# Folding the last quarter of a down projection into seven half-size products, in a hybrid encoder layer on one core

## The chip, the core and the metric

The kernel runs on one core of one Trainium2 chip. A core has a TensorE for matrix products (PE in the profile, PEld for its weight loads), a VectorE (DVE), a ScalarE (ACT), a GpSimd (POOL) and a SyncE (SP), which here only issues DMA transfers. Products are accumulated in the eight banks of PSUM; everything else lies in SBUF, in 83 slots of 128 x 512 fp32 and some smaller buffers. The metric is the device time of one execution in microseconds, lower is better.

## The reference, cut to what matters

One layer, 512 tokens by 1024 channels, fp32. The first half (norm, one input projection, a two-direction state-space scan, windowed attention, gates, an output projection) is not changed in what it computes, and only small edits of the diff touch it. The second half is the channel mixing:

```
h = rmsnorm(x, pre_mlp_norm)
f = square(relu(h @ w_mlp_in)) @ w_mlp_out      # w_mlp_in 1024 x 4096, w_mlp_out 4096 x 1024
x = x + rmsnorm(f, post_mlp_norm)
```

## The kernel before

**Three passes for a product.** A matrix product in near-fp32 precision is made of three passes in a rounded 32-bit type: both operands are split into a high part (rounded, by ACT) and a low part (the difference, by DVE or POOL), and `mm3` (L404) multiplies high by high, high by low and low by high into one bank. Weights come by DMA into raw tiles; ACT makes the high part (L473, or L1474 for the folded products) and POOL the low part in pieces of 256 columns (L477, L1477). Three buffers hold split weights (`SPL`).

**Quanta.** The program is a list of quanta (`Quantum`, L332), each a group of matmuls with its chunks of weights; `run_quanta` (L502) loads and splits ahead. `at(q, fn)` (L427) places other work beside quantum q. The instructions written out this way are then put in order by a planner (`Planner`, L92). It takes their dependences, an estimated cost for each, and due times counted back from the TensorE's own order (`deadlines`, L246), plays the program through, and fixes each engine's order with dependences (`chain`, L489). `depend` (L164) treats every two accesses to one PSUM bank as ordered, and also makes the first use of a tile wait for the first use of the tile that held the buffer's tag before. `next_matmul` (L126) tries to stay with one kind of matmul, since going from 128-wide to 64-wide tiles costs time. The 64-wide kind are pairs that write the two halves of a bank; the scan's `yd` (L1100 on) and the attention values use them.

**The MLP.** The up projection has 32 quanta of 24 matmuls, one for each block of 128 hidden channels (`up_quantum`, L1396; `up_done`, L1336, takes relu and square). The down projection is done by quarters of the hidden dimension. In a quarter the product is 512 tokens x 1024 hidden by 1024 hidden x 1024 outputs. Seen as 2 x 2 blocks, it takes eight block products directly, or seven with sums of blocks:

```
A (2x2) by B (2x2):  S2 = A21 + A22 - A11, S1 = A21 + A22, S3 = A11 - A21, S4 = A12 - S2
                     T2 = B22 - B12 + B11, T1 = B12 - B11, T3 = B22 - B12, T4 = T2 - B21
```

Here token halves are A's rows and output halves are B's columns. Each block product is 24 matmuls of 128 x 128 by 128 x 512 (two row blocks u of 128 tokens, four k, three passes). The first three quarters (`FOLDED = 3`) do it with seven products (`folded_quanta`, L1427 on). `combine` (L1362) makes the sums of A from two up blocks, `operand` the sums of B on DVE, from raw weight tiles. Three of the seven share a bank X and add up in it, two share Y, and A12 (bank Z) and A22 with T4 (bank W) have one to themselves. After each product `gather` (L1506 on) adds the bank into the outputs' accumulators `acc` (L1512), with a minus for A22 T4. Between the seven products of a quarter lie the up quanta of the next.

**The last quarter** has no up quanta left. It is unfolded (`down_quanta`, L1514 on): two output halves j, each four row blocks t by 24 matmuls, 192 matmuls for the two, the last row block of the second half in two pieces of 256 columns (24 more, shorter, matmuls). Its weights come as eight chunks of 512 KB. `down_done` (L1548 on) finishes a row block: add `acc` (L1557), square and sum on ACT (L1559), the running mean on DVE (L1562, L1564), the product with the norm's gain (`ag`, L1568), the power -1/2 on POOL (L1571), the scaled sum with x (L1575) and the store (L1576).

**Three places further ahead.** At the start 10 and then 8 matmuls on zeros run on TensorE while the inputs land (`WARM`), with the turn of a gain vector between them. `dt_math` (L718) evaluates log(1 + e) by a series with terms to 1/19. `k_done` (L786) splits K and writes each part to both halves of the partitions; both copies of the low part are made from the bank.

## Time and profile before

| | |
|---|---|
| median of 3 runs | 1101.49 us (1101.03 to 1101.82) |
| the profiled execution's own time | 1102.23 us |
| its span, from the first to the last instruction | 1100.4 us |
| granted TensorE clock, mean | 0.999 |
| DVE, ACT, POOL busy | 65%, 57%, 70% |
| bytes moved, mean rate | 128.12 MB, 116 GB/s |

The span is what the profile's clock covers; the execution's own time has 1.8 us more around it. "Busy" of an engine is a share of the span. Matmuls overlap: each row of one shows a length of about 0.39 us, but they start 0.227 us apart, so rates are read from starts. An idle time in square brackets behind a row is the time that the engine stood before it, with the work that ended it.

### The profile page before, as it was taken

Reading aid. Unit: us, or ns where it says so; the run is one execution under the profiler, and the core shown is the slowest. Engines: PE = TensorE matmul, PEld = TensorE weight load, DVE = VectorE, ACT = ScalarE, POOL = GpSimd, SP = SyncE. Lnnn points to the kernel's source line nnn. Section 1 sums busy time; section 2 is a strip of 40 time slices with the busy share of each in tenths; the row PEclk is TensorE's granted clock in tenths of the full one; section 3 lists DMA queues with packets and bytes.
Section 4 is the critical chain, followed back from the end, with each engine's and each line's share of the span. In section 5 each row is a group of like instructions: output and inputs, shape, how many; then the busy total and the mean of one; then the engine's idle time right before and its main releaser. Section 6 shows DMA issues by size and latency. Waiting matters only on the chain.

```text
span 1100.4 us, 16692 instructions
## 1 busy us (share of the span) xinstructions
PE 1087.9 (99%) x5679; PEld 912.4 (83%) x5679; DVE 710.3 (65%) x1242; ACT 627.2 (57%) x1345; POOL 771.0 (70%) x944
## 2 busy tenths in 40 slices
PE   9999999999999999999999999999999999999997
PEld 8878888888888878888888888889888888888886
DVE  5577787688687687777887753434655556564236
ACT  6466677677777667586779532323555444444331
POOL 3546667557668788898999776511679889898841
PEclk9999999999999999999999999999999999999999
DMA  7434434543454536354645564513312522523232
GB/s 203 126 94 111 117 92 111 140 106 101 114 123 124 145 96 168 97 148 126 165 129 148 142 171 125 170 53 98 113 39 77 172 58 78 171 58 97 64 108 77
DMA packets 206921, 128.12 MB, mean 116 GB/s; under 512 B 10170, under 2 KB 191930, under 8 KB 206835
## 3 DMA queue, kind: packets, MB, share of 16 engines
q1 hardware_dynamic: 206675, 126.98, 41.7%
q8 instruction: 45, 0.74, 0.3%
q14 instruction: 41, 0.34, 0.1%
q10 hardware_dynamic: 160, 0.07, 0.0%
HBM read 124.60 MB, written 2.42 MB: 115 GB/s over the span
## 4 chain that ended last, share of the span: by engine, by line
PE 63%; DVE 1%; issue 0%; ACT 0%; POOLq 0%; POOL 0%; DVEq 0%
PE pp L398 46%; PE ps L398 16%; PE ps L402 1%; DVE m L1095 0%; DVE m L1094 0%; DVE x L1575 0%; DVE rf L1089 0%; ACT junk L1559 0%; DVE acc L1557 0%; POOLq L1656 0%; POOL frs L1571 0%; DVE cb L1083 0%; DVEq L1656 0%; DVE frs L1564 0%; DVEq L1095 0%
## 5 line engine op out<-in xcount | busy, mean ns | idle before, releaser
L477 POOL TENSOR_TENSOR wl<-wr,wh 128x256 fp32r<-128x256 f32 (+1 forms) x511 | 442.0, 894 | 188.4 <-ACT wh L473 180.0
L398 PE MATMUL pp<-h,wh 128*128 128x512 f32 (+1 forms) x1728 | 527.9, 388 | 1.7 <-DVE KL L794 1.7
L398 PEld LDWEIGHTS pp<-h,wh 128*128 128x128 f32 x1728 | 319.1, 188 | 66.7 <-issue 4.2
L398 PE MATMUL pp<-h,wl 128*128 128x512 f32 (+1 forms) x856 | 332.1, 388 | 0.0
L473 ACT CAST wh<-wr 128x1024 fp32r<-128x1024 f32 (+1 forms) x141 | 146.9, 1043 | 162.7 <-PE pp L398 111.4
L398 PEld LDWEIGHTS pp<-h,wl 128*128 128x128 f32 x856 | 160.8, 188 | 32.1 <-issue 0.2
L1477 POOL TENSOR_TENSOR wl<-wd,wh 128x256 fp32r<-128x256 f32 x144 | 117.1, 849 | 13.6 <-ACT wh L1474 12.2
L398 PE MATMUL ps<-wl,fh 128*128 128x512 f32 (+1 forms) x192 | 73.0, 380 | 0.0
L398 PE MATMUL ps<-wh,fl 128*128 128x512 f32 (+1 forms) x192 | 73.0, 380 | 0.0
L398 PE MATMUL ps<-wh,fh 128*128 128x512 f32 (+1 forms) x192 | 73.0, 380 | 0.0
L1092 ACT ACTIVATE n<-cb,tables 128x128 f32<-128x128 f32 x128 | 49.1, 392 | 20.5 <-DVE cb L1083 17.8
L1474 ACT CAST wh<-wd 128x512 fp32r<-128x512 f32 x72 | 41.5, 619 | 31.3 <-PE ps L398 19.8
L924 DVE SCALAR_TENSOR_TENSOR u<-pp,cv,u 128x510 f32<-128x510 f32 (+1 forms) x64 | 47.7, 745 | 7.8 <-ACT u L920 6.7
L1088 ACT ACTIVATE rf<-rf,tables 128x128 f32<-128x128 f32 x128 | 42.5, 393 | 15.1 <-DMA rf<-csT 15.0
L398 PE MATMUL pp<-yh,wl 128*128 128x512 f32 x128 | 49.8, 390 | 0.0
L398 PE MATMUL pp<-yl,wh 128*128 128x512 f32 x128 | 49.6, 389 | 0.0
L398 PE MATMUL pp<-yh,wh 128*128 128x512 f32 x128 | 49.6, 389 | 0.0
L1093 ACT ACTIVATE m<-cb,tables 128x128 f32<-128x128 f32 x128 | 48.8, 390 | 0.2 <-DVE cb L1083 0.2
L856 ACT ACTIVATE P<-P,mx 128x384 f32<-128x384 f32 (+1 forms) x64 | 35.3, 553 | 20.7 <-DVE mx L853 20.5
L1022 POOL TENSOR_TENSOR xd<-x,tables 128x256 f32<-128x256 f32 x48 | 33.2, 712 | 16.1 <-ACT x L947 12.8
L1086 POOL TENSOR_TENSOR rb<-rb,tables 128x512 f32<-128x512 f32 x32 | 35.1, 1099 | 11.5 <-DMA rb<-csT 11.3
L398 PEld LDWEIGHTS ps<-wl,fh 128*128 128x128 f32 x192 | 36.1, 188 | 7.1
(257 smaller groups left out, 2064.9 us busy)
## 6 DMA issues: line engine op xcount, KB each, us to landing
wr<-in_w_in SPq DMA_DIRECT2D x76, 512.0 KB, 4.2
wr<-in_w_mlp_in SPq DMA_DIRECT2D x32, 512.0 KB, 4.2
wd<-in_w_mlp_out SPq DMA_DIRECT2D x48, 256.0 KB, 3.4
rf<-csT SPq DMA_DIRECT2D x32, 256.0 KB, 4.3
rb<-csT SPq DMA_DIRECT2D x32, 256.0 KB, 5.3
wr<-in_w_ssd_out SPq DMA_DIRECT2D x14, 512.0 KB, 5.1
E<-csE SPq DMA_DIRECT2D x96, 64.0 KB, 3.6
x<-in_x SPq DMA_DIRECT2D x16, 256.0 KB, 6.0
```

Source lines behind the costliest of these rows:

```text
L398: self.nc.tensor.matmul(out, lhsT, rhs, start=start, stop=stop, skip_group_check=more)
L473: self.nc.scalar.copy(hi[:, :m], raw)
L477: engines[e].tensor_tensor(lo[:, c], raw[:, c], hi[:, c].bitcast(F32), op=ALU.subtract)
L856: nc.scalar.activation(p[:, :w], p[:, :w], AF.Exp, bias=mx[:, n:n + 1], accum_out=sm[:, n:n + 1])
L924: nc.vector.scalar_tensor_tensor(u[:, a:e], ps[:, a + d:e + d], self.wtap(t, b), u[:, a:e], op0=ALU.mult, op1=ALU.add)
L1022: nc.gpsimd.tensor_tensor(v4(xd[:, d * 256:(d + 1) * 256]), v4(xs(c)), by_dir(self.coef, c)[:, d].unsqueeze(2).to_broadcast([128, 4, 64]), ...
L1086: nc.gpsimd.tensor_tensor(v4(rb), v4(rb), cs[:, 1].unsqueeze(2).to_broadcast([128, 4, 128]), op=ALU.subtract)
L1088: nc.scalar.activation(v4(rf)[:, h], v4(rf)[:, h], AF.Identity, bias=ncs[:, 0, h:h + 1])
L1092: nc.scalar.activation(v4(n)[:, h], cb[:, 0], AF.Copy, scale=dt[:, 0, h:h + 1])
L1093: nc.scalar.activation(v4(m)[:, h], cb[:, 1], AF.Copy, scale=dt[:, 1, h:h + 1])
L1474: nc.scalar.copy(hi[:, cols], src)
L1477: (nc.vector if q == 512 else nc.gpsimd).tensor_tensor(lo[:, c], src[:, e * q:(e + 1) * q], hi[:, c].bitcast(F32), op=ALU.subtract)
```

## The change

The last quarter goes through `folded_quanta` too; `down_quanta` and the unfolded branch of `up_done` are gone. In all quarters T4 is made with the other sign, so that A22's product adds into bank X as the fourth, and the bank W and the subtraction are gone. The order of the seven is A11, S2, S3, S1, A22, S4, A12 in the first three quarters, and A11, A12, S2, S1, S4, S3, A22 in the last. S3's product is gathered only into (1,1), since (1,0) takes the same bank after A22. In the last quarter the sixteen weight tiles are loaded by `at`, three to five quanta before the quarter begins, and half of each T sum's low part goes to DVE as 512 columns (`LAST_LO`). `down_done` runs after the last gather into each output block, in whatever order they complete.

Beside that, the planner starts a 64-wide matmul only when everything that its bank's matmuls wait for is done, if something else is ready (`awaited`), and a buffer's order rule holds only where no other dependence does (`after`). The zero matmuls at the start stand in one row of 18, the series stops at 1/17, and the second copy of K's low part is copied by ACT from the first.

```diff
-FOLDED = 3
-WARM = 10, 8
+LAST_LO = dict(LO, **{n: [LO[n][0], [(0, 512)]] for n in ('T1', 'T2', 'T3', 'T4')})
+WARM = 18
...
+        self.awaited, banks = {}, {}
+        for n, k in enumerate(self.kind):
+            if k and k[1]:
+                banks.setdefault(self.operands(self.ins[n].outs)[0].tensor.name, []).append(n)
+        for bank in banks.values():
+            needed = set().union(*(self.pre[n] for n in bank)) - set(bank)
+            self.awaited.update((n, needed) for n in bank)
...
-    def next_matmul(self, some, ready, t, kind):
+    def next_matmul(self, some, ready, done, t, kind):
         now = sorted(n for n in some if ready[n] <= t)
+
+        now = [n for n in now if all(done[m] <= t for m in self.awaited.get(n, ()))] or now
...
-                                self.turn[n].add(first[held[-2]])
+                                after[name] = first[held[-2]]
...
-                    if name in base and not any(u in self.pre[n] for u, *_ in live[name]):
-                        self.pre[n] |= base[name]
+                    if not any(u in self.pre[n] for u, *_ in live[name]):
+                        self.pre[n] |= base.get(name, set())
+                        if name in after:
+                            self.turn[n].add(after[name])
...
-        for _ in range(WARM[0]):
+        for _ in range(WARM):
             self.mm(pg[:, 128:256], zero, zero, True, True)
...
-        for _ in range(WARM[1]):
-            self.mm(self.dummy[:, :128], zero, zero, True, True)
...
-        nc.vector.tensor_scalar(p, s2, 1.0 / 19, None, op0=ALU.mult)
-        for n in (17, 15, 13, 11, 9, 7, 5, 3):
+        nc.vector.tensor_scalar(p, s2, 1.0 / 17, None, op0=ALU.mult)
+        for n in (15, 13, 11, 9, 7, 5, 3):
...
                 nc.scalar.copy(KH[b], ps[a])
-                nc.vector.tensor_tensor(KL[b], ps[a], KH[a].bitcast(F32), op=ALU.subtract)
+                nc.scalar.copy(KL[b], KL[a])
...
             if name == "T4":
                 t = raw["B11", k]
-                tt(t, t, raw["B21", k], op=ALU.subtract)
-                return t, (("B11", k), ("B21", k))
-            return raw[name, k], (("B22", k),) if name == "B22" else ()
+                tt(t, raw["B21", k], t, op=ALU.subtract)
+                return t, (("B11", k),) + ((("B21", k),) if order.index("A12") < order.index("A22") else ())
+            done = name == "B22" or name == "B21" and order.index("A12") > order.index("A22")
+            return raw[name, k], ((name, k),) if done else ()
...
-                    for e, q in LO[name][n]:
+                    for e, q in (LAST_LO if part == 3 else LO)[name][n]:
...
-        def product(a, b, bank, first, done):
+        def product(a, b, bank, first, to):
             def run(parts):
+                end = first and part == 3 and a == order[-1]
                 if first:
-                    banks[bank] = [self.bank("ps") for _ in range(2)]
+                    banks[bank] = [self.bank("pp" if part == 3 and bank == "Z" else "ps") for _ in range(3 if end else 2)]
                 for u in range(2):
                     tok = slice(u * 128, (u + 1) * 128)
...
+                    for col in [slice(0, 256), slice(256, 512)] if end and u else [slice(0, 512)]:
+                        ps = banks[bank][u + (col.start > 0)]
+                        for k in range(4):
+                            hi, lo = self.f[part, k][a]
+                            wh, wl = parts[k // 2]
+                            self.mm3(ps[:, col], (hi[:, tok], lo[:, tok]), (wh[:, k % 2, col], wl[:, k % 2, col]),
+                                     first and k == 0, k == 3, not first)
+                        for t, j in to:
+                            self.gather(2 * t + u, j, ps, col)
+                            if part == 3 and a == [p for p in order if (t, j) in products[p][3]][-1]:
+                                if not self.complete:
+                                    self.g4 = self.norm_rows("post_mlp_norm")
+                                self.down_done(2 * t + u, j, col)
...
+        products = {"A11": ("B11", "X", True, [(0, 0)]), "S2": ("T2", "X", False, [(0, 1)]), "S3": ("T3", "X", False, [(1, 1)]),
+                    "A22": ("T4", "X", False, [(1, 0)]), "S1": ("T1", "Y", True, [(1, 1)]), "S4": ("B22", "Y", False, [(0, 1)]),
+                    "A12": ("B21", "Z", True, [(0, 0)])}
+        if part == 3:
+            for name, lead in (('B11', 4), ('B22', 4), ('B12', 4), ('B21', 3)):
+                for k in range(4):
+                    self.at(len(self.quanta) - lead - (k < 2), lambda name=name, k=k: load(name, k))
+        order = ('A11', 'A12', 'S2', 'S1', 'S4', 'S3', 'A22') if part == 3 else ("A11", "S2", "S3", "S1", "A22", "S4", "A12")
+        return [product(a, *products[a]) for a in order]
...
-        nc.vector.tensor_tensor(a, ps[:, col], a, op=ALU.add)
...
-        if j == 1 and col.stop == 512:
+        if sum(c.stop - c.start for _, c in seen) == D:
             r = rs[:, n % 2:n % 2 + 1]
             nc.gpsimd.tensor_tensor(r, r, self.mhalf, op=ALU.pow)
-            for i in range(2):
+            for i, c in seen:
                 x1 = self.x1[t][i]
-                for c in [slice(0, 512)] if t < 3 or i == 0 else [slice(0, 256), slice(256, 512)]:
-                    nc.vector.scalar_tensor_tensor(x1[:, c], self.ag[t, i][:, c], r, x1[:, c], op0=ALU.mult, op1=ALU.add)
-                    nc.sync.dma_start(self.out[0, t * 128:(t + 1) * 128, i * 512 + c.start:i * 512 + c.stop], x1[:, c])
+                nc.vector.scalar_tensor_tensor(x1[:, c], self.ag[t, i][:, c], r, x1[:, c], op0=ALU.mult, op1=ALU.add)
+                nc.sync.dma_start(self.out[0, t * 128:(t + 1) * 128, i * 512 + c.start:i * 512 + c.stop], x1[:, c])
...
-        for part in range(FOLDED):
+        for part in range(4):
             down = self.folded_quanta(part)
+            if part == 3:
+                self.add(*down)
+                break
             for i in range(8):
                 self.add(*down[i:i + 1], self.up_quantum(8 * part + 8 + i))
-        for j in range(2):
-            self.add(*self.down_quanta(3, j))
```

More of the change, by code (lines that the diff above doesn't have):

```diff
@@ L165, in depend @@
         self.pre = [set() for _ in self.ins]
-        live, users, ring, seen, first, base = {}, {}, {}, {}, {}, {}
+        live, users, ring, seen, first, base, after = {}, {}, {}, {}, {}, {}, {}
         self.turn = [set() for _ in self.ins]
@@ L266, in plan @@
         ready = [0.0] * len(self.ins)
+        done = [math.inf] * len(self.ins)
         avail = {e: [] for e in self.OVERLAP}
@@ L285, in plan @@
             if e == "PE":
-                n = self.next_matmul(some, ready, t, kind)
+                n = self.next_matmul(some, ready, done, t, kind)
             else:
@@ L316, in plan @@
                 free[e] = end - self.OVERLAP[e]
+            done[n] = end
             for s in self.post[n]:
@@ L575, in start @@
         pg = self.bank("ps")
-        for _ in range(WARM[0]):
+        for _ in range(WARM):
             self.mm(pg[:, 128:256], zero, zero, True, True)
+        put(zero)
         self.tr(pg[:, :8], g[:8, :])
@@ L581, in start @@
         self.dummy = self.bank("ps")
-        for _ in range(WARM[1]):
-            self.mm(self.dummy[:, :128], zero, zero, True, True)
-        put(zero)
         self.h = [(get("h", dtype=F32R), get("h", dtype=F32R)) for _ in range(8)]
@@ L1393, in block @@
         part, n = divmod(i, 8)
-        return i if part >= FOLDED else 8 * part + n // 2 + 4 * (n % 2)
+        return 8 * part + n // 2 + 4 * (n % 2)
     def up_quantum(self, i):
@@ L1466, in loads @@
                     for k in ks:
-                        load(n, k)
+                        if (n, k) not in raw:
+                            load(n, k)
             def make():
@@ L1498, in product, with gather @@
             return Quantum([chunk(b, c) for c in range(2)], run)
-        add, sub = ALU.add, ALU.subtract
-        return [product("A11", "B11", "X", True, [(0, 0, add)]), product("S2", "T2", "X", False, [(0, 1, add)]),
-                product("S3", "T3", "X", False, [(1, 0, add), (1, 1, add)]), product("S1", "T1", "Y", True, [(1, 1, add)]),
-                product("S4", "B22", "Y", False, [(0, 1, add)]), product("A12", "B21", "Z", True, [(0, 0, add)]),
-                product("A22", "T4", "W", True, [(1, 0, sub)])]
-    def gather(self, t, j, ps, op):
+        products = {"A11": ("B11", "X", True, [(0, 0)]), "S2": ("T2", "X", False, [(0, 1)]), "S3": ("T3", "X", False, [(1, 1)]),
[7 more added lines that the diff above has]
+        return [product(a, *products[a]) for a in order]
+    def gather(self, t, j, ps, col):
         if (t, j) not in self.acc:
@@ L1511, in gather, with down_done @@
         else:
[L1512 to L1548 removed]
+            a = self.acc[t, j][:, col]
+            self.nc.vector.tensor_tensor(a, a, ps[:, col], op=ALU.add)
+    def down_done(self, t, j, col):
         nc = self.nc
[L1551 to L1552 removed]
+        if not self.complete:
             self.fs = self.tmp("fsq", [128, 4, 3], 1), self.tmp("frs", [128, 8], 1)
+        seen = self.complete.setdefault(t, [])
+        n = len(seen)
+        seen.append((j, col))
         ssq, rs = self.fs[0][:, t], self.fs[1][:, 2 * t:2 * t + 2]
[L1555 removed]
         a = self.acc[t, j][:, col]
[L1557 removed]
         junk = self.slots.get("junk")
```

65 lines of the change are left out of this document (10 added, 55 removed).

## The prediction

> **What bounds the kernel now.** I read the page's busy table first, then the list of what the TensorE waited for, then the chain of waits backwards from the end, and last the timeline of the stages that the diff touches.
>
> ```profile
> span 1100.4 us, 16692 instructions
> PE 1087.9 (99%) x5679; PEld 912.4 (83%) x5679; DVE 710.3 (65%) x1242; ACT 627.2 (57%) x1345; POOL 771.0 (70%) x944
> ...
> PE pp L398 <- DVE KL L794: 1.7, 1, 1.7
> PE ps L398 <- DVE m L1095: 1.2, 2, 0.7
> ```
>
> TensorE (PE) is busy 99% of the span, and the two waits shown are the largest it has. So a product taken away shortens the run by its own length, unless its weights or its sums come late afterwards. The chain of waits gives the length of a product in the down projection:
>
> ```profile
> 875.81 10.88 PE pp L398 x48
> 886.69 5.44 PE ps L398 x24
> ...
> 1033.59 5.44 PE ps L398 x24
> 1039.03 10.88 PE pp L398 x48
> 1049.91 21.76 PE ps L398 x96
> 1071.67 4.08 PE pp L398 x18
> 1075.75 1.43 PE ps L398 x12
> 1077.18 12.28 PE pp L398 x54
> ...
> 1089.06 0.39 PE L398 MATMUL pp<-wh,fl 128*128 128x512 f32 x1
> ...
> 1093.48 0.28 PE L398 MATMUL ps<-wh,fl 128*128 128x256 f32 x1
> ```
>
> The first two rows are a handover that the kernel has already: two up products, and then the first folded product, without a gap. The third is the last folded product of the third quarter: 24 matmuls in 5.44 us, 0.2267 us each. The fourth is the last two up products; the rest is the unfolded last quarter, from 1049.91 to the end of its last matmul at 1093.48 + 0.28 = 1093.76.
>
> **The change part by part.** I work against the profiled execution (1102.23 us, of which the span is 1100.4), and apply the difference to the median of the three runs, 1101.49.
>
> *The products.* Last quarter before: 43.85 us (1093.76 - 1049.91). After: seven products of 24 matmuls, 7 x 5.44 = 38.08, and the last matmul, 512 wide, ends 0.39 - 0.23 = 0.16 us behind its slot: 38.24. This takes away **5.6 us** of the bounding engine. The up products before it stay the same 24 matmuls each. The first product, A11, needs only the even up result; A12 needs the last odd one 5.44 us later. The handover at 886.69 is the same and has no gap, so I cost it at nothing; A12's cover is the 5.44 us of A11.
>
> *The end.* After the last matmul comes a chain on DVE, ACT and POOL.
>
> ```profile
> 1085.41 0.69 DVE L1557 TENSOR_TENSOR acc<-pp,acc 128x512 f32<-128x512 f32 x1 [0.37 <-PE pp L398]
> ...
> 1087.71 1.41 DVE L1575 SCALAR_TENSOR_TENSOR x<-ag,frs,x 128x512 f32<-128x512 f32 x2 [0.66 <-POOL frs L1571]
> ...
> 1093.17 0.75 DVE L1575 SCALAR_TENSOR_TENSOR x<-ag,frs,x 128x512 f32<-128x512 f32 x1
> 1093.84 0.42 DVE L1557 TENSOR_TENSOR acc<-ps,acc 128x256 f32<-128x256 f32 x1
> ...
> 1095.65 1.54 DVE L1575 SCALAR_TENSOR_TENSOR x<-ag,frs,x 128x512 f32<-128x512 f32 x3 [0.66 <-POOL frs L1571]
> ```
>
> Before, the last piece is 256 columns: from 1093.76 to 1095.65 + 1.54 = 1097.19, 3.43 us. After, `end` in the product is never true (A22 is not a first write of its bank), so the last piece is a whole 512: the full-width chain in the first two rows takes 1087.71 + 1.41 - 1085.41 = 3.71 us, plus 0.04 from the matmul's end. That is 0.3 more. Its two row blocks also come closer: half a product, 2.72 us, apart, while each chain is 3.71 long, so the last addition meets the two 0.75 us output steps of the block before it on DVE. Between 0 and 2 x 0.75; I take 0.4, since only one of them can be ahead of it. The last store is 256 KB where it was 128; no row separates the two, 0 to 0.3, I take 0.1. Together **+0.8** (0.3 to 2.1).
>
> *Weights.* In the last quarter no up product lies between the folded ones any more. Each product needs two chunks of weights split: ACT rounds, POOL (or DVE) takes the difference.
>
> ```profile
> 1027.58 5.63 POOL L1477 TENSOR_TENSOR wl<-wd,wh 128x256 fp32r<-128x256 f32 x8
> ...
> L1477 POOL TENSOR_TENSOR wl<-wd,wh 128x256 fp32r<-128x256 f32 x136 | 110.4, 848 | 9.9 <-ACT wh L1474 8.4 <-DVE fs L1380 1.0
> L1474 ACT CAST wh<-wd 128x512 fp32r<-128x512 f32 x68 | 39.0, 620 | 27.6 <-PE ps L398 19.8 <-PE pp L398 6.9 <-POOL wl L477 0.7
> L1445 DVE TENSOR_TENSOR wd<-wd,wd 128x512 f32<-128x512 f32 x8 | 5.7, 711 | 0.0
> ...
> 875.75 4.78 POOL L477 TENSOR_TENSOR wl<-wr,wh 128x256 fp32r<-128x256 f32 x4 [1.48 <-ACT wh L473]
> 876.35 1.23 DVE L416 TENSOR_TENSOR fl<-fs,fh 128x512 fp32r<-128x512 f32 x1
> ```
>
> Undisturbed, eight differences take POOL 5.63 us, 0.70 each, against 5.44 us of matmuls; at the stage's mean of 0.848 they take 6.8. Where a DVE operation with both operands in SBUF falls in, both stretch: four differences took 4.78 instead of 2.82, and the DVE one beside them 1.23 where its kind takes 0.71. So the plain blocks (B11, B21, B22) cost POOL 5.6 to 6.8 us for a product of 5.44; the four sums T cost POOL half of that, 2.8 to 3.4, because `LAST_LO` gives every second one to DVE. B11 is split under the up products. The tight place is the second chunk of B21, then of B22: its buffer comes free 18 matmuls (4.08 us) into the product before, then 0.62 on ACT and 4 x 0.70 on POOL make 7.5; PE takes the last of it at 5.44 + 9 x 0.227 + 0.23 = 7.7. One DVE operation in between makes PE wait. Lower bound 0; upper bound 2 x (6.8 - 5.44) = 2.7 at the stage's mean. I take 0.5 at each, **+1.0**: the rest of each chunk's split is nearer to the undisturbed row, but the T sums run just then.
>
> The Trainium skill, page "SBUF — State Buffer", section "Who interferes with whom", says that a DVE instruction with two SBUF inputs and a GpSimd instruction that reads SBUF exclude each other for the whole instruction, so that work moved from one to the other gains little. Taken strictly it would put T's product at 4 x 0.70 + 2 x 0.71 = 4.2 us of the pair instead of 2.8, and makes the first rival below likelier. The row of 4.78 agrees: 1.96 us more than the same four take undisturbed.
>
> ```profile
> wd<-in_w_mlp_out SPq DMA_DIRECT2D x48, 256.0 KB, 3.4
> L1512 DVE TENSOR_TENSOR acc<-acc,ps 128x512 f32<-128x512 f32 x40 | 26.9, 682 | 15.8 <-PE ps L398 15.8
> ```
>
> The sixteen weight loads of the last quarter move four to five quanta ahead; at 3.4 us to land they are there 15 us before their use, and they let T2's first subtractions run under the up products. They replace eight loads of the same bytes. On SP they stand in front of the last up products' loads, whose ring of three holds two products (10.9 us) of cover: nothing, or one late load, 0 to 1 us; I take 0. Joining the fourth sum to the shared bank drops two additions per quarter, six of 0.68 us on DVE, in stretches where PE never waited: 0. Before the next product may write into that bank the additions must have read it; the other row block's 2.72 us covers one of 0.68. The folded inputs of the last quarter cost DVE and ACT what the first three did, under the same up products, without a PE wait: 0.
>
> *The smaller edits.* The second copy of the low part of K moves to ACT:
>
> ```profile
> 56.15 0.69 DVE L792 TENSOR_TENSOR KL<-pp,KH 64x512 fp32r<-64x512 f32 x1
> 56.88 0.59 ACT L793 CAST KH<-pp 64x512 fp32r<-64x512 f32 x1 [0.54 <-DVE KL L792]
> ...
> 57.49 0.28 PE L398 MATMUL ps<-KL,Q 128*128 128x256 f32 x1
> ...
> 58.60 0.69 DVE L794 TENSOR_TENSOR KL<-pp,KH 64x512 fp32r<-64x512 f32 x1
> ...
> 59.44 0.70 PE L398 MATMUL pp<-h,wh 128*128 128x512 f32 x2 [1.67 <-DVE KL L794]
> ```
>
> PE stood 1.67 us because a PSUM bank was read last by L794, which DVE reached only at 58.60. After, the bank is done with when ACT ends L793, 57.47. What is late next: PE itself was busy to 57.8. **-1.6** (0 if the new order brings another reader there, to -1.7). The shortened series takes one DVE step away in the same stretch: in this.
>
> The planner's two new rules reorder the whole program. The one on paired matmuls waits until all that a bank needs is there.
>
> ```profile
> 392.37 0.66 PE L398 MATMUL ps<-m,x 128*64 128x128 f32 x8 [0.56 <-DVE m L1095]
> 393.68 0.66 PE L398 MATMUL ps<-m,x 128*64 128x128 f32 x8 [0.65 <-DVE m L1095]
> ...
> 457.96 0.59 PE ps L398 x8
> ...
> 610.65 1.02 PE ps L398 x16
> ```
>
> Here PE began eight and then eight, waiting 0.56 and 0.65 us. That wait, 1.2, is what the rule aims at. Eight take 0.59 and sixteen 1.02, so a visit to such matmuls costs 2 x 0.59 - 1.02 = 0.16 beside its work; a few merged or split visits move a few tenths. From -2.4 (the wait and some eight visits merged) to +1.5 (as many split, another wait); I take the wait alone, **-1.2**.
>
> ```profile
> 1.03 5.06 PE L398 MATMUL ps<-zero 128*128 128x128 f32 x22 [1.03 <-DVE mhalf L569]
> ...
> 6.23 1.87 PE L398 MATMUL ps<-zero 128*128 128x128 f32 x14
> ...
> 8.98 1.04 PE L402 MATMUL pp<-ident,x 128*128 128x128 f32 x8
> ```
>
> The eighteen idle matmuls at the start become one row of the same count, ending near 8.1 as now, before x is there at 8.98: 0, at most 0.3 if DVE's gT copy, now after them, holds up x's scaling.
>
> Sum: -5.6 + 0.8 + 1.0 - 1.6 - 1.2 = **-6.6 us**. The profiled run would come to 1095.6; the median, 0.74 lower than the profiled run before, to **1094.9**.
>
> **The rivals.** *Supply binds over the whole last quarter.* From the start of A11, POOL has 32 differences (22.5 us) and DVE some 19 SBUF operations (T1 and T4 four each, one of T2's, eight differences, two of the last folded inputs: 19 x 0.71 = 13.5 us) and the output's eight first scalings (8 x 0.71 = 5.7). If they hardly overlap, that is 36 to 42 us for weights that PE wants 6 x 5.44 + 2.04 = 34.7 us in. For it: the 4.78 row. Against it: half-size POOL work for four of seven products, and PE unhindered where POOL is at its 0.848 mean. At 5 us of waits instead of 1: 1094.9 + 4 = 1098.9.
>
> *Slower: POOL alone falls behind on the plain blocks.* Place: A12 and S4, as above; each waits 8d - 5.44 for a difference of d us. Without the 1.0 taken, the sum is -7.6, so it turns at 2 x (8d - 5.44) = 7.6, d = 1.155. At 1.23, the time the stretched DVE row had, each wait is 4.4 and the run 1094.9 + 7.8 = 1102.7. Against it: the mean of 136 in the folded stage is 0.848.
>
> *The time does not change, because the new order loses elsewhere what the products give.* The rules touch every matmul's place. To lose 6.6 us, every saving of the small edits must fail (2.8) and some 24 visits be split (3.8): about 1101.5. For it: nothing in the rows; against it: the rules make matmuls wait for what they need together, which takes waits away sooner than it adds them.
>
> **How the numbers follow.** Forecast 0.71, supply over the whole quarter 0.14, POOL behind 0.07, order loses 0.08. The bounds of the terms add up to -5.6 + 0.3 + 0 - 1.7 - 2.4 = -9.4, or 1092.1, at the low end, so low is 1092.0. The high end takes in the first rival and part of its spread, 1099.6; the other two lie outside. What this kernel's measurement can tell from no change is about 0.2%, 2.2 us: faster means below 1099.3. Of the first rival three quarters lie there, and a little of the third: faster 0.82, same 0.10, slower 0.08.
>
> **What would show it.** Right: seven blocks of 5.44 us behind the last two up products; PE idle in the last quarter of about 1 us, named POOL or DVE `wl` and lying in A12 and S4; no PE wait on KL; the last matmul ending near 1086 in the span (1049.91 - 2.8 + 38.2 + 1.0) and some 4.2 us from its end to the last output step. Wrong: PE waits of 3 us or more in the last quarter, waits on a PSUM reader (`acc`) between products, a new wait on a weight load, or blocks before 1040 that stand later than now.

## The result, and the profile after

| | before | after |
|---|---|---|
| median of 4 runs each, same chip | 1101.29 us (1101.03 to 1101.82) | 1095.43 us (1094.15 to 1096.77) |
| ratio | | 0.9947, interval 0.9934 to 0.9960 |
| the profiled execution's own time | 1102.23 us | 1094.15 us |
| its span | 1100.4 us | 1092.1 us |

The change takes 5.9 us away (forecast 6.6, to 1094.9). The profiled executions lie 8.1 us apart, because that of before is 0.9 above its median and that of after 1.3 below its own. So a step read from the two traces can look up to 2.2 us larger than it is in the medians, and one step does (the start, below).

The page of after, its busy table:

```profile
span 1092.1 us, 16762 instructions
...
PE 1080.2 (99%) x5631; PEld 904.9 (83%) x5631; DVE 742.0 (68%) x1288; ACT 641.0 (59%) x1379; POOL 793.8 (73%) x977
```

Its list of what TensorE waited for (us in total, times, longest):

```profile
PE ps L411 <- DVE wl L1483: 0.7, 1, 0.7
...
PE ps L411 <- DVE pT L884: 0.3, 1, 0.3
```

TensorE still bounds the kernel up to its last stretch. The waits on `KL` (1.7) and on the scan's `m` (1.2) are gone; a new one stands in their place, on a low part of weights that DVE makes. The chain of waits of after, first the quarters and then the end:

```profile
798.87 5.44 PE ps L411 x24
...
1043.74 5.44 PE ps L411 x24
...
1054.62 3.87 PE ps L411 x17
...
1060.10 1.85 DVE wd L1460 x2
1061.95 1.15 DVE wl L1483
...
1063.15 13.23 PE ps L411 x56
...
1076.48 0.54 ACT wh L1480
...
1077.71 0.76 DVE wl L1483
...
1087.44 1.32 DVE x L1559 x2
```

Against the rows of before: the first folded product comes at 798.87 instead of 805.09 (-6.22). From there to the last quarter's A11 nothing moves (244.87 us, before 244.82). The last matmul is this one:

```profile
1082.88 0.39 PE L411 MATMUL ps<-wh,fc 128*128 128x512 f32 x1
```

It ends at 1083.27, so the last quarter takes 39.53 us (1083.27 - 1043.74) instead of 43.85: 38.24 of products as forecast, and 1.29 of waits. In the last quarter the chain leaves TensorE twice: in S1, where DVE operations stand between two matmuls, and at 1076.38 (1063.15 + 13.23), 6.9 us before the last matmul ends; from 1077.71 on it runs mostly through DVE. The timeline around the first, DVE and then TensorE:

```profile
1059.42 0.67 DVE L1531 TENSOR_TENSOR acc<-acc,ps 128x512 f32<-128x512 f32 x1
1060.02 1.93 DVE L1460 TENSOR_TENSOR wd<-wd,wd 128x512 f32<-128x512 f32 x2
1061.87 1.22 DVE L1483 TENSOR_TENSOR wl<-wt,wh 128x512 fp32r<-128x512 f32 x1
```

```profile
1062.03 0.39 PE L411 MATMUL ps<-wh,fh 128*128 128x512 f32 x1
1063.15 0.50 PE L411 MATMUL ps<-wl,fh 128*128 128x512 f32 x1 [0.73 <-DVE wl L1483]
```

Starts of matmuls are 0.227 apart when nothing waits; here they are 1.12 apart. DVE made two of the sums for T4, which nobody needed yet, before T1's low part, which TensorE was waiting for. Beside POOL's differences such an operation takes 0.97 to 1.22 us here (1.93 / 2, 1.22), not the 0.71 that I used.

The end, DVE's timeline of after:

```profile
1081.91 0.74 DVE L1559 SCALAR_TENSOR_TENSOR x<-ag,frs,x 128x512 f32<-128x512 f32 x1
...
1083.30 0.69 DVE L1531 TENSOR_TENSOR acc<-acc,ps 128x512 f32<-128x512 f32 x1
1084.03 0.69 DVE L1553 TENSOR_TENSOR ag<-acc,post_mlp_norm 128x512 f32<-128x512 f32 x1
1084.63 0.74 DVE L1559 SCALAR_TENSOR_TENSOR x<-ag,frs,x 128x512 f32<-128x512 f32 x1
1085.30 0.15 DVE L1549 SCALAR_TENSOR_TENSOR frs<-fsq,frs 128x1 f32<-128x1 f32 x1
1085.37 3.39 DVE L1559 SCALAR_TENSOR_TENSOR x<-ag,frs,x 128x512 f32<-128x512 f32 x5
```

The last addition is not late: it begins at 1083.30, 0.03 behind the last matmul. But none of the eight output steps comes before 1081.91, and six of them stand behind the last matmul. The powers for the first two row blocks were done on POOL at 1076.81 and their products with the gain on DVE at 1077.02, so four of the eight steps had been waiting for DVE alone since then. Of the six behind the last matmul, one delays the last mean (`frs`, 1085.30), and then five run in a row to 1088.76, the last row block's two behind three others. So the end takes 5.49 us (1088.76 - 1083.27), not 3.43. The busy times by engine show why DVE is behind; the columns are the window and its length, then PE, PEld, DVE, ACT and POOL (us, instructions), the granted clock, the DMA share and GB/s. Before and after, from a few us ahead of the last quarter:

```profile
1046.00:1100.40 54.40, 47.76 (x234) 40.32 (x232) 27.33 (x41) 13.86 (x27) 16.05 (x10) 0.98 0.27 91
```

```profile
1040.00:1092.10 52.10, 42.53 (x185) 33.97 (x183) 45.25 (x68) 21.59 (x46) 37.48 (x40) 0.94 0.11 41
```

DVE was busy half of this stretch (27.33 of 54.40), and is now busy 87% of it (45.25 of 52.10). Busy counts the whole length of an operation, also what it is stretched by beside POOL.

### The profile page after: what moved, and what is told of

The parts are those of the page before. It is cut to its first block, busy times and chain, and to the rows that moved or that the text cites. A ratio compares the mean times of both kernels' runs of the same rounds, so it can differ in the third digit from the quotient of the medians.

```text
span 1092.1 us, 16762 instructions
## 1 busy us (share of the span) xinstructions
PE 1080.2 (99%) x5631; PEld 904.9 (83%) x5631; DVE 742.0 (68%) x1288; ACT 641.0 (59%) x1379; POOL 793.8 (73%) x977
## 4 chain that ended last, share of the span: by engine, by line
PE 71%; DVE 1%; issue 0%; ACT 0%; DVEq 0%; ACTq 0%
PE pp L411 51%; PE ps L411 18%; PE ps L415 1%; DVE x L1559 0%; DVE acc L1531 0%; DVE ag L1553 0%; DVE wl L1483 0%; DVE wd L1460 0%; DVE m L1105 0%; DVE pT L884 0%; ACT junk L1544 0%; DVEq L1641 0%; DVE m L1106 0%; ACT wh L1480 0%; DVE frs L1547 0%
## 5 line engine op out<-in xcount | busy, mean ns | idle before, releaser
L490 POOL TENSOR_TENSOR wl<-wr,wh 128x256 fp32r<-128x256 f32 (+1 forms) x504 | 423.7, 869 | 154.5 <-ACT wh L486 143.5
L486 ACT CAST wh<-wr 128x1024 fp32r<-128x1024 f32 (+1 forms) x133 | 138.4, 1041 | 148.0 <-PE pp L411 117.3
L1483 POOL TENSOR_TENSOR wl<-wd,wh 128x256 fp32r<-128x256 f32 x180 | 151.3, 875 | 16.5 <-ACT wh L1480 16.5
L1480 ACT CAST wh<-wd 128x512 fp32r<-128x512 f32 x96 | 55.3, 618 | 39.2 <-PE ps L411 19.3
L411 PE MATMUL ps<-wl,fh 128*128 128x512 f32 x184 | 71.6, 391 | 0.7 <-DVE wl L1483 0.7
L411 PE MATMUL ps<-wh,fl 128*128 128x512 f32 x184 | 71.3, 389 | 0.0
L411 PE MATMUL ps<-wh,fh 128*128 128x512 f32 x184 | 71.0, 389 | 0.0
L1355 DVE SCALAR_TENSOR_TENSOR pp<-pp,r 128x512 f32<-128x512 f32 (+1 forms) x31 | 17.6, 567 | 66.8 <-ACT r L1352 66.8
L1139 POOL TENSOR_TENSOR w<-w,E 128x256 f32<-128x256 f32 x48 | 38.4, 813 | 13.0 <-DVE w L1135 11.6
```

Of the source, the lines that this page charges most:

```text
L411: self.nc.tensor.matmul(out, lhsT, rhs, start=start, stop=stop, skip_group_check=more)
L486: self.nc.scalar.copy(hi[:, :m], raw)
L490: engines[e].tensor_tensor(lo[:, c], raw[:, c], hi[:, c].bitcast(F32), op=ALU.subtract)
L1139: nc.gpsimd.tensor_tensor(wc, wc, E[:, d], op=ALU.add)
L1480: nc.scalar.copy(hi[:, cols], src)
L1483: (nc.vector if q == 512 else nc.gpsimd).tensor_tensor(lo[:, c], src[:, e * q:(e + 1) * q], hi[:, c].bitcast(F32), op=ALU.subtract)
```

## The experiments

Each was timed several times beside the kernel before on the same chip (medians of before 1101.27 to 1101.57). Their intervals are about 0.0013 wide to each side, 1.4 us, so medians closer than that are not told apart by them, and there the trace has to speak.

**1. The two halves of the change apart.** First, `main_alone`: the fold of the last quarter with its loads and the shared bank, without the small edits.

```diff
-WARM = 18
+WARM = 10, 8
...
-        now = [n for n in now if all(done[m] <= t for m in self.awaited.get(n, ()))] or now
...
-                                after[name] = first[held[-2]]
+                                self.turn[n].add(first[held[-2]])
...
-        nc.vector.tensor_scalar(p, s2, 1.0 / 17, None, op0=ALU.mult)
+        nc.vector.tensor_scalar(p, s2, 1.0 / 19, None, op0=ALU.mult)
...
-                nc.scalar.copy(KL[b], KL[a])
+                nc.vector.tensor_tensor(KL[b], ps[a], KH[a].bitcast(F32), op=ALU.subtract)
```

> The folded last quarter with its early loads and the shared bank, but the start, the series, the copy of K's low part and the planner's two rules as before. Theory (from the two traces): the products give 4.3 us and the end takes 2.2 back, so about 2.1 us under the kernel before, near 1099.2. Rival (the prediction's own terms): 5.6 less 1.0 of waits less 0.8 at the end, 3.8 us under, near 1097.5.

Measured: 1098.80 us (nine executions, 1098.51 to 1099.83; a tenth took 2206.79 and is left out), ratio 0.9979 (0.9970 to 0.9989). Its list of waits, its A11 in the chain, and DVE's end:

```profile
PE pp L407 <- DVE KL L803: 1.7, 1, 1.7
...
PE ps L407 <- DVE wl L1481: 0.7, 1, 0.7
PE ps L407 <- DVE m L1104: 0.7, 1, 0.7
```

```profile
1049.66 5.44 PE ps L407 x24
```

```profile
1091.27 3.40 DVE L1557 SCALAR_TENSOR_TENSOR x<-ag,frs,x 128x512 f32<-128x512 f32 x5
```

A11 stands where it stood before (1049.66, before 1049.91), with the waits on `KL` and on `m` (0.7 here, 1.2 before). The wait on DVE's `wl` and the five output steps in a row belong to the fold. It is worth 2.3 us by the ratio and 2.5 by the medians, where my terms for it add up to 3.8 (-5.6 + 0.8 + 1.0); the interval, 1.2 to 3.3 us, leaves that out.

Then `small_alone`: the other half, those edits (the shorter series too) made to the kernel before, whose last quarter stays unfolded.

```diff
-WARM = 10, 8
+WARM = 18
...
+        now = [n for n in now if all(done[m] <= t for m in self.awaited.get(n, ()))] or now
...
-                                self.turn[n].add(first[held[-2]])
+                                after[name] = first[held[-2]]
...
-                nc.vector.tensor_tensor(KL[b], ps[a], KH[a].bitcast(F32), op=ALU.subtract)
+                nc.scalar.copy(KL[b], KL[a])
```

> The last quarter as before, unfolded, with all the small edits: one row of 18 zero matmuls, the shorter series, the copy on ACT, the planner's rules. Theory: these edits give most of the time: 1.7 us for K, some 2.8 for the planner's rules, and up to 1.7 at the start, so 4.5 to 6.2 us under the kernel before, 1095.1 to 1096.8. Rival (the prediction): 2.8 us, near 1098.5, with nothing at the start.

Measured: 1096.77 us (1095.89 to 1097.60), ratio 0.9957 (0.9944 to 0.9971). The small edits are worth 4.5 us, where I had 2.8; here too the interval, 3.2 to 6.2, leaves my figure out. The halves add up to 7.0, the whole gives 5.9; the spreads cover that. So the forecast was near by luck: one half gives 1.3 to 1.5 us less than I had, the other 1.7 more.

**2. The start.** `old_start`: the zero matmuls as 10 and 8 again.

```diff
-WARM = 18
+WARM = 10, 8
...
-        for _ in range(WARM):
+        for _ in range(WARM[0]):
...
+        for _ in range(WARM[1]):
+            self.mm(self.dummy[:, :128], zero, zero, True, True)
```

> The changed kernel with 10 and 8 zero matmuls again. Theory: the gain vector's copy stands ahead of the first sum of squares on DVE again and waits for the turn behind ten cold matmuls, so the turns of x start near 9.0 us instead of 7.3, the span of the profile is about 1.7 us over 1092.1, and the runs lie closer together than the 2.6 us of the changed kernel. Rival: the start is worth nothing, the same 1095.4 with the same spread.

Measured: 1095.39 us (1094.79 to 1096.15), ratio 0.9944 (0.9932 to 0.9957): the median is that of the whole change, with a narrower spread. DVE's start in the kernel before, in the one after, and after's first transposes of x on TensorE:

```profile
6.34 0.17 DVE L579 COPY gT<-ps 128x8 f32<-128x8 f32 x1 [5.35 <-PE ps L402]
6.42 0.68 DVE L608 CUSTOM_DVE_ANT_0 junk<-x 128x512 f32<-128x512 f32 x1
```

```profile
4.75 0.69 DVE L619 CUSTOM_DVE_ANT_0 junk<-x 128x512 f32<-128x512 f32 x1 [3.76 <-DMA x<-in_x]
...
6.93 0.17 DVE L593 COPY gT<-ps 128x8 f32<-128x8 f32 x1
```

```profile
7.32 1.04 PE L415 MATMUL pp<-ident,x 128*128 128x128 f32 x8
```

The edit does something I had not seen. Before, the first sum of squares stood on DVE behind gT, which waits for ten zero matmuls; after, it starts when x lands. In the profiled execution the transposes come 1.66 us earlier for it (7.32 instead of 8.98); with the old start they are at 8.93. But a faster start is a gain only if nothing further on takes it back, and the medians do not show it. What remains of it is below what these times can tell.

**3. DVE's backlog.** `no_gain` leaves the eight products with the norm's gain out.

```diff
-        if col.start == 0:
-            self.ag[t, j] = self.slots.get("ag")
-        nc.vector.tensor_tensor(self.ag[t, j][:, col], a, self.g4[j][:, col], op=ALU.mult)
...
-                nc.vector.scalar_tensor_tensor(x1[:, c], self.ag[t, i][:, c], r, x1[:, c], op0=ALU.mult, op1=ALU.add)
+                nc.vector.scalar_tensor_tensor(x1[:, c], self.acc[t, i][:, c], r, x1[:, c], op0=ALU.mult, op1=ALU.add)
```

> The changed kernel without the eight products with the last norm's gain (ag); the output step takes the unscaled sum, so the output lacks that gain. DVE has 8 x 0.7 us less, none of them in the last chain from matmul to store. Theory (DVE's backlog sets the end): from the last matmul's end to the last output step about 3.8 us instead of 5.5, 1.3 to 2 us under the changed kernel, near 1093.8. Rival (the end is the length of its own chain): 5.3 to 5.5 us, within 0.5 us of the changed kernel.

Measured: 1092.64 us (1091.40 to 1093.34), ratio 0.9918 (0.9904 to 0.9931), 2.8 us less than the change, with an interval that lies below the change's. Its last matmul and DVE's end:

```profile
1081.51 0.39 PE L411 MATMUL ps<-wh,fc 128*128 128x512 f32 x1
```

```profile
1081.93 0.69 DVE L1531 TENSOR_TENSOR acc<-acc,ps 128x512 f32<-128x512 f32 x1 [0.40 <-PE ps L411]
1082.54 1.41 DVE L1556 SCALAR_TENSOR_TENSOR x<-acc,frs,x 128x512 f32<-128x512 f32 x2
...
1084.67 1.42 DVE L1556 SCALAR_TENSOR_TENSOR x<-acc,frs,x 128x512 f32<-128x512 f32 x2 [0.66 <-POOL frs L1553]
```

With some 5.5 us less on DVE (eight of 0.683), the output steps of the earlier row blocks are done in time, DVE stands idle again before its last two, and the end falls to 4.2 us (1084.67 + 1.42 - 1081.90). The wait in S1 is gone as well: no wait on `wl` is in its list of waits. Less work on DVE takes both away. That leaves one rival open: the planner puts the instructions in a new order in every run, and in the changed kernel DVE stands idle for 0.69 us before 1077.71, although the output steps of two row blocks were ready. No run keeps the work and changes only the order at the end.

**4. The same work on POOL.** `lows_on_pool` gives the eight low parts back to POOL.

```diff
-LAST_LO = dict(LO, **{n: [LO[n][0], [(0, 512)]] for n in ('T1', 'T2', 'T3', 'T4')})
+LAST_LO = LO
```

> The changed kernel with all low parts of the last quarter's T sums on POOL (LAST_LO = LO): DVE loses 8 operations of 0.7 to 1.2 us there, POOL gets 16 more of 0.70. Theory A (DVE's backlog sets the end): from the last matmul to the last output step it takes at least 1 us less than 5.5, while PE waits for POOL grow by 1 to 3 us; 1095 to 1097.5. Theory B (the end is the length of its own chain): the 5.5 stay, the wait on a DVE low part of 0.9 in S1 goes and others on POOL come.

Measured: 1107.89 us (1106.11 to 1108.17), ratio 1.0052 (1.0039 to 1.0065): slower than before. Neither theory had it. DVE, POOL and then TensorE:

```profile
1073.36 1.37 DVE L1531 TENSOR_TENSOR acc<-acc,ps 128x512 f32<-128x512 f32 x2 [4.63 <-PE ps L411]
1074.64 9.15 DVE L1553 TENSOR_TENSOR ag<-acc,post_mlp_norm 128x512 f32<-128x512 f32 x1
```

```profile
1067.28 15.97 POOL L1483 TENSOR_TENSOR wl<-wd,wh 128x256 fp32r<-128x256 f32 x23
```

```profile
1079.05 0.39 PE L411 MATMUL ps<-wh,fl 128*128 128x512 f32 x1
1085.28 0.77 PE L411 MATMUL ps<-wh,fc 128*128 128x512 f32 x1 [5.84 <-DVE acc L1531]
```

One `ag`, 0.69 us by itself, took 9.15, and ended 0.54 us behind the last of 23 differences that POOL ran without a pause (0.694 each). The additions behind it on DVE free the bank that TensorE needs, so two matmuls start 6.23 us apart. Of the 12 us between the two traces, 10.0 lie before the end of the last matmul (1093.24 against 1083.27) and 2.0 behind it (7.51 against 5.49). A long row on POOL is not enough for this, though. Earlier in the same trace, POOL and then DVE:

```profile
1048.56 11.16 POOL L1483 TENSOR_TENSOR wl<-wd,wh 128x256 fp32r<-128x256 f32 x12 [0.74 <-ACT wh L1480]
```

```profile
1059.05 1.22 DVE L1553 TENSOR_TENSOR ag<-acc,post_mlp_norm 128x512 f32<-128x512 f32 x1
```

Beside this row of twelve, and at the start of the next, which follows without a pause, the two engines took turns: the twelve took 0.93 each, and an `ag` got through in 1.22. What made the difference at 1074.64 the runs do not show, nor whether half of the low parts on DVE helps because it breaks up POOL's row or because it shares the load.

**5. The wait in S1 by itself.** `t1_low_pool` gives only T1's low parts to POOL; `t1_from_raw` makes T1's sum early, from raw tiles, ahead of the others.

```diff
-LAST_LO = dict(LO, **{n: [LO[n][0], [(0, 512)]] for n in ('T1', 'T2', 'T3', 'T4')})
+LAST_LO = dict(LO, **{n: [LO[n][0], [(0, 512)]] for n in ('T2', 'T3', 'T4')})
```

> The changed kernel with T1's low parts all on POOL (LAST_LO without T1). Theory: the wait of 0.9 us in S1, where T1's second low part queued behind two T4 sums on DVE, goes, and DVE's backlog is two operations shorter, so 1 to 2 us under the changed kernel. Rival: POOL's longer rows shut DVE out as they did with all lows on POOL, and new waits on DVE take it back: the same or up to 3 us slower.

```diff
+                if part == 3:
+                    raw["T1", k] = get("wt")
+                    tt(raw["T1", k], b, c, op=ALU.subtract)
...
-                raw["T1", k] = get("wt")
-                tt(raw["T1", k], raw["B22", k], raw["B11", k], op=ALU.subtract)
+                if part < 3:
+                    raw["T1", k] = get("wt")
+                    tt(raw["T1", k], raw["B22", k], raw["B11", k], op=ALU.subtract)
```

> The changed kernel with the last quarter's T1 made as B12 - B11 from the raw tiles, ahead of T2's sums in place, so that its four sums can run as soon as the loads land. Theory: they move from 1041 to 1051 us to before that, DVE is less behind from A12 on, the wait in S1 shrinks and the end is up to 2 us shorter: 0.5 to 2.5 us under the changed kernel. Rival: DVE's place in the row is set by due times, not by when the tiles are there: the same time.

Measured: 1095.80 us (1094.09 to 1096.22; ratio 0.9945, 0.9933 to 0.9958) and 1096.32 us (1095.50 to 1097.21; ratio 0.9952, 0.9939 to 0.9966). In both the gap of 1.12 is gone and nothing is won. In the first, TensorE has four places instead where starts lie 0.47 to 0.58 apart; in the second there is one of 0.71 at 1051.17 and one of 0.80 at 1068.15, and DVE's row at the end is longer:

```profile
1086.31 4.72 DVE L1563 SCALAR_TENSOR_TENSOR x<-ag,frs,x 128x512 f32<-128x512 f32 x7
```

All late starts of matmuls in the last quarter add up to 1.87 and 1.61 us in these two traces, and to 1.27 in that of the change. In these two runs another order, or a part of the work given to POOL, moved DVE's wait and did not remove it.

**6. Work taken off DVE.** `rows01` gives the four output steps of row blocks 0 and 1 to ACT (scaling) and POOL (adding x); `rows01_warm16` has 16 zero matmuls beside that (`WARM = 16`).

```diff
-                nc.vector.scalar_tensor_tensor(x1[:, c], self.ag[t, i][:, c], r, x1[:, c], op0=ALU.mult, op1=ALU.add)
+                if t < 2:
+                    nc.scalar.activation(self.ag[t, i][:, c], self.ag[t, i][:, c], AF.Copy, scale=r)
+                    nc.gpsimd.tensor_tensor(x1[:, c], x1[:, c], self.ag[t, i][:, c], op=ALU.add)
+                else:
+                    nc.vector.scalar_tensor_tensor(x1[:, c], self.ag[t, i][:, c], r, x1[:, c], op0=ALU.mult, op1=ALU.add)
```

> The four output steps of row blocks 0 and 1 leave the VectorE: the ScalarE scales, the GpSimd adds x; everything else is as in the changed kernel. Theory (the VectorE's backlog sets the end): in the changed kernel the last row block's mean waits 0.55 us behind an output step, and three of five output steps in a row stand before its two; with four steps gone the end falls from 5.5 us behind the last matmul to about 4.2, so 1093.8 to 1094.4. Rival: the GpSimd additions, some 1.4 us each, shut the VectorE's steps with both operands in SBUF out, and the power of row block 2 or 3 queues behind them: 1095.4 or more, end 5.5 us or longer.

> As the one before, and 16 zero matmuls at the start instead of 18, so that the turn of the gain vector follows earlier when the full clock comes late; the gain's copy on the VectorE still stands behind both scalings of x. Theory (the changed kernel's spread of 2.6 us comes from executions in which the row of 18 ends after x is there): 0.3 to 0.8 us less than the run before in the median, and a narrower spread. Rival: the start does not decide the median, as undoing it altogether had shown: the same within 0.3 us, and the same spread.

Measured: 1094.75 us (1094.26 to 1095.32; ratio 0.9938, 0.9926 to 0.9951) and 1095.01 us (1093.80 to 1095.58; ratio 0.9937, 0.9923 to 0.9951). Both lie a little under the change's 1095.43, with intervals that overlap its own, so neither is shown to be faster; two zero matmuls less make no difference that these times can tell. The time of the first lies between those of its theory and its rival; its trace says that the end is not shorter. POOL and then DVE:

```profile
1079.51 6.03 POOL L1561 TENSOR_TENSOR x<-x,ag 128x512 f32<-128x512 f32 x4
1085.63 1.60 POOL L1556 TENSOR_TENSOR frs<-frs,mhalf 128x1 f32<-128x1 f32 x2
```

```profile
1084.41 1.14 DVE L1549 SCALAR_TENSOR_TENSOR frs<-fsq,frs 128x1 f32<-128x1 f32 x1
...
1086.75 2.73 DVE L1563 SCALAR_TENSOR_TENSOR x<-ag,frs,x 128x512 f32<-128x512 f32 x4
```

The last matmul ends at 1083.77 and DVE at 1089.48: 5.7 us, as the rival said. The mean of one column, 0.14 to 0.16 us in most rows, took 1.14 beside POOL's additions, and the last two powers stood behind them until 1085.63.

**7. The planner's rules.** `no_awaited` takes out the rule on paired matmuls, `no_after` the new form of the buffer's rule, `no_rules` both; the edits are these.

```diff
-        now = [n for n in now if all(done[m] <= t for m in self.awaited.get(n, ()))] or now
```

> The changed kernel without the one line that keeps a 64-wide matmul back until all that its bank needs is done (the other planner rule stays). Theory: the visits to 64-wide matmuls rise from 24 to 30 again and the waits on the scan's sums come back: 1.5 to 2.8 us slower than the changed kernel. Rival: the other rule made the new order: within 0.5 us.

```diff
-                                after[name] = first[held[-2]]
+                                self.turn[n].add(first[held[-2]])
...
-                    if not any(u in self.pre[n] for u, *_ in live[name]):
-                        self.pre[n] |= base.get(name, set())
-                        if name in after:
-                            self.turn[n].add(after[name])
+                    if name in base and not any(u in self.pre[n] for u, *_ in live[name]):
+                        self.pre[n] |= base[name]
```

> The planner's rule on a buffer's order goes back to its old form (the first use of a tile waits for the first use of the tile that had the buffer before, always); the rule on paired matmuls stays. Without the other rule the time stayed within 0.3 us although the visits to 64-wide matmuls went back from 24 to 30. Theory A: the buffer's order rule is what let the scan's and the attention's work come earlier, about 2.85 us in the profiled run less what the visits are worth: 1097.5 to 1098.5 here, the first matmul of the last quarter's A11 some 2 us later than 1043.7. Theory B: either rule by itself is enough for most of it: 1095.4 to 1096.2 here, A11 at 1044 to 1045.

> Both of the planner's rules go back to their old form; nothing else of the change is undone. Each undone by itself left the time within 0.3 us of the changed kernel on its chip; the last quarter's A11 came 1015.6 us behind the start of the dt quantum without the rule on paired matmuls and 1014.4 without the new buffer rule, 1014.3 with both, 1018.8 in the kernel before. Theory A (each rule alone is enough, the two together are worth about 2.7 us, since 1.7 of the 4.5 are K's copy): 1097.3 to 1098.2, A11 about 1017 behind the dt quantum, the waits at 392 us back. Theory B (the buffer rule does nothing here, the rule on paired matmuls about 1): 1095.4 to 1096.4, A11 about 1015.6 behind.

Measured: 1095.73 us (1095.32 to 1098.52; ratio 0.9951, 0.9939 to 0.9964), 1094.36 us (1094.23 to 1095.94; ratio 0.9939, 0.9927 to 0.9952) and 1096.89 us (1096.23 to 1099.94; ratio 0.9964, 0.9950 to 0.9978). By the medians either rule alone is enough: `no_awaited` is 0.3 us slower than the change, as its rival said of the time, and `no_after` 1.1 faster, below both of its theories. Without both the kernel is 1.5 us slower, between the two theories, with an interval that overlaps the change's. The trace without both rules: the list of waits, TensorE's timeline, and the chain:

```profile
PE ps L407 <- DVE m L1102: 0.3, 1, 0.3
```

```profile
30.57 1.20 PE L407 MATMUL pp<-h,wh 128*128 128x512 f32 x4
...
390.18 0.66 PE L407 MATMUL ps<-m,x 128*64 128x128 f32 x8 [0.33 <-DVE m L1102]
```

```profile
1046.46 5.44 PE ps L407 x24
```

The last quarter begins 1015.89 us behind the dt quantum (1046.46 - 30.57); with both rules it is 1014.33 (1043.74 - 29.41), before 1018.82. It is 1015.52 without the rule on pairs (1044.98 - 29.46) and 1014.39 without the buffer's (1044.03 - 29.64), so by the traces nearly all of the 1.6 us belongs to the rule on pairs, which the medians do not show. The matmuls of 64 columns are visited 30 times without that rule, as before, and 24 times with it. Of the wait at 392 us, 1.2 before, only 0.3 returns without both rules and nothing without the rule on pairs, so most of it went by other changes of the order: in `main_alone`, with neither rule, it is 0.7 already.

## Why the prediction was right, and where it was not

The time (1094.9 against 1095.43), the direction and the range held. That the time came so near is luck, as experiment 1 shows. By its steps:

| step | forecast | shown |
|---|---|---|
| products | -5.6 | -5.6: 38.24 of the 39.53 us are products |
| waits on weights | +1.0 | +1.29, at another place |
| the end | +0.8 (0.3 to 2.1) | +2.06 (5.49 - 3.43), the same in `main_alone` |
| the K copy | -1.6 | -1.7, the wait is gone and none follows it |
| the planner's rules | -1.2 | -1.5 in the medians, `no_rules` against the change; the intervals overlap |
| the start | 0 | -1.7 in the profiled executions, 0 in the medians |
| sum | -6.6 | -5.9 in the medians; the rows above do not add up to it |

*Products, K:* right, mechanism and size. No run undoes the K copy alone, but its wait is in none of the traces that keep it (`no_rules`, `old_start`), and it is in `main_alone`.

*Rules:* the size is near, within a spread that is as large as they are; the mechanism was wrong. I took the wait at 392 us as what the rule on pairs saves, but without that rule the wait does not return. What does return are six visits, an estimated 1.0 us (6 x 0.16, the prediction's estimate for one), and in the trace the last quarter begins 1.2 us later for it (1015.52 against 1014.33). The median of that run is only 0.3 slower, so what the six visits cost is not shown.

*Waits on weights:* the size was near, the place and the engine were wrong. I took POOL's plain blocks, 8 x 0.70 against 5.44, in A12 and S4. There TensorE did not wait. It waited in S1 for DVE, which I had costed at 0.71 an operation with both operands in SBUF and which took up to 1.23 beside POOL. The numbers for this stood in the first rival: some 19 such operations. I did not carry them over to the end of the kernel. I also read the row of 4.78 as POOL's with one DVE operation in it; the trace has four beside it.

*The end:* this is the term that was mis-sized, and the step behind it is "the last addition meets the two 0.75 us output steps of the block before it on DVE". The addition meets none. What is late are output steps: DVE still has six of the eight to do when the last matmul ends. `no_gain` bears this out: less work on DVE takes 2.8 us away, 1.3 of it in the end (5.49 to 4.2) and 0.9 in the last quarter (1043.25 to 1081.90, 38.65 instead of 39.53). The 4.2 is my 3.43 + 0.8 in number only: there two output steps, from 1082.54 to 1083.95, hold up the last mean and not the addition.

*The small edits:* as a whole they are worth 4.5 us and not 2.8. K's 1.7 and the rules' 1.5 leave 1.3 that no run here gives to one edit. The traces show pieces of it (the rest of the wait at 392 us, 0.3 of the wait on `pT`), and the start in some executions. The start I had put at nothing, since I read 8.98 as the time at which x is there; x was there by 6.42, when DVE begins its sum of squares. How these share the 1.3 stays open.

The rivals: supply did bind, on DVE, but cost 1.3 us in waits and 1.3 in the end (2.06 against 0.8), not 5. POOL alone did not fall behind. A mechanism that makes this kernel slower than before exists, though, and I did not name it: one DVE operation held up behind POOL for 9.15 us, in a run that is 12.5 us slower than the change for one line (experiment 4).

## What to carry to other kernels

When a product is folded away, cost the work that it moves to the other engines over the whole stretch, to its very end: here DVE was busy for 87% of it, and what it had not done in time reappeared after the last matmul, where nothing hides it. Another order, or work handed to its neighbour, only moved its waits in the runs above; in the one run with less work for all engines together (`no_gain`) they were gone. And undo the two halves of a change apart before a forecast that came out near is believed, since here errors of 1.3 to 1.5 and of 1.7 us cancelled.

## What the runs showed of the hardware

*DVE behind POOL.* I had taken contention as a factor of at most 1.7 (1.23 us beside 0.71). In `lows_on_pool` one operation took 9.15 us, while POOL went from one difference to the next. The Trainium skill, page "SBUF — State Buffer", section "Who interferes with whom", says that a DVE instruction with two SBUF inputs contends with a GpSimd instruction that reads SBUF, that the contention is an exclusive lock, and that issue order decides who blocks. The rows agree with the exclusion (1.22 us instead of 0.69 for an `ag` that took turns with POOL); that a row of instructions can keep DVE out for 13 of them (9.15 / 0.694) is what they add. It is one event in one trace, and the row of twelve at 1048.56 did not do it.

*The clock after a wait.* The windows of `lows_on_pool` (columns as above):

```profile
1079.00:1084.00 5.00, 0.44 (x2) 0.01 (x1) 5.00 (x3) 0.00 (x0) 4.30 (x8) 0.92 0.00 0
1084.00:1091.00 7.00, 5.72 (x15) 4.55 (x16) 3.15 (x8) 1.33 (x4) 1.37 (x2) 0.57 0.00 0
```

No matmul starts between 1079.05 and 1085.28; in the second stretch the granted clock is 0.57. From 1085.28 to 1090.10 the matmuls start 0.427 us apart (the first two 0.564) instead of 0.227. Over these 4.8 us the rate is about half, so this wait of 6 us was paid again by some 2.3 us. No other run here has a gap of that length between matmuls.
